# A two-layer hybrid trunk on one core: its instructions ordered by the context's timeline simulator

## The chip, the cores and the metric

The kernel runs on one core of one Trainium2 chip. The metric is the device time of one execution in microseconds; the median of several runs counts. A core has engines that run side by side, each with its own queue of instructions, which it takes in the order in which the program put them there: PE multiplies matrices (PEld is its weight load), ACT computes activations and copies, DVE does elementwise work, POOL does a little of that, and SP issues DMAs. An instruction that waits for another engine holds up what stands behind it in its own queue.

## The reference

Two decoder layers over 256 tokens of width 1024, all in float32. Cut to what matters:

```python
for l in range(2):
    x = layer_norm(ALPHA * x + swiglu_half(x, ffn1_w1[l], ffn1_w3[l], ffn1_w2[l]), ln1_g[l], ln1_b[l])
    h = x @ w_in[l]                                   # columns for three token mixers
    out_a = spatial_gating(gelu(a_u), gelu(a_v), ...)
    out_b = gated_deltanet(b_qkv, b_z, b_beta, b_decay, ...)   # short conv, triangular solve, recurrence
    out_c = gla(c_q, c_k, c_v, c_r, c_g, ...)                  # chunked recurrence
    mix = concatenate([out_a, out_b, out_c], axis=-1) @ w_out[l]
    x = layer_norm(ALPHA * x + mix, ln2_g[l], ln2_b[l])
    x = layer_norm(ALPHA * x + swiglu_half(x, ffn2_w1[l], ffn2_w3[l], ffn2_w2[l]), ln3_g[l], ln3_b[l])
# swiglu_half(x, w1, w3, w2) = 0.5 * ((silu(x @ w1) * (x @ w3)) @ w2), inner width 2816
```

## The kernel before

The activations live in SBUF as `x`, transposed: 8 blocks of 128 features by 256 tokens. All weights come from HBM as "units" of 128x1024 floats, 167 for a layer, through a ring of `raw` tiles that SP fills by DMA. Most units are split into two tiles of a narrower float: ACT casts `raw` to `wh` (L209), and DVE subtracts to get the rest, `wl` (L210). The activations are split in the same way into a high part (`xH`, or `gs` for the second FFN product) and a low part. Each 128x128 block of a unit is then three matmuls in `mm3`: `wh` by the high part (L242), `wh` by the low part (L243), `wl` by the high part (L244), 256 or 258 columns each. Units named in `whole` are used as float32 at once (L323).

A layer is FFN1, a layer norm, the mixer, a layer norm, FFN2, a layer norm. An FFN block `f` makes two products `h` (from w1 and w3), ACT and DVE turn them into `gs`, and three blocks later the products `y` (four banks of PSUM, y_0 to y_3) add the block's part of the output. PSUM has these four, and two banks each under the tags "h" and "c" for everything else.

A layer norm is spread over engines. `ln_open` adds `y` to `x` (L353) and at once makes a raw split of `x`, not yet normalised, so that PE can go on with units of the next stage whose result is corrected afterwards ("raw" products: in front of the mixer these are `pmisc`, `pm`, `pz` and `pr`; in front of an FFN, some `h`). Sums of `x` and of its square end in two matmuls `pst` (L401), and from these `ln_stats` makes the scale `rs` in a chain between ACT and DVE: `muN` (ACT, L409), its square (ACT, L410), the variance (DVE, L411 and L412), a logarithm and an exponential (ACT, both recorded as L170), and one refining step (DVE, L415 to L417). Then `x` is normalised: DVE takes off the mean (L421) and multiplies by `rs` (L425), ACT applies gain and bias (L429, `ln_x`), and `split` makes the high part (ACT, L247) and the low part (DVE, L248). The first products that use the normalised `x` are `pk` in the mixer, and `h` of a later block in an FFN. A raw product is copied out of PSUM by ACT (L629, into `zrm`), and corrected by DVE (L635, L637).

The mixer is a string of short steps on all engines between units of its own: projections (`pk`, `pq`, `pv`, each with a short convolution, L614 and L616, or by `pcv` matmuls, L680), norms of q and k (`pss`, L747), gate sums (`ptr`, L805), a triangular solve whose result is transposed on DVE (`iv`, L882 and L883), its use in small matmuls (`p1a` L899, `p2a` L905, `p1b` L919), a recurrence, and the output product.

Nothing in the code writes out the queues. `trunk` issues instructions in an order of its own, with `ahead(n)` as a priority in places. The context that it runs in (`tile.TileContext`, opened at L1346) collects them, decides in which order they stand in each engine's queue, gives them tile slots, and adds the semaphores. It picks the next instruction among those whose inputs are due by an estimate of time, and by priority.

## Time and profile before

| | us |
| --- | --- |
| median of 3 runs | 1071.11 (1066.88 to 1072.26) |
| the profiled execution | 1075.11 |
| its span, first to last instruction | 1073.3 |
| PE busy in it | 1047.1 (98%) |
| DVE busy | 749.8 (70%) |
| ACT busy | 601.4 (56%) |

The span is what the trace shows; the remaining 1.8 us lie around it. Busy shares are of the span. The granted clock of TensorE ("PEclk") is a share of its full 2.4 GHz; 0.5 is the other level, 1.2 GHz.

### The profile page before, as it was taken

What the parts mean: (1) busy time and instruction counts of PE and PEld (TensorE: products, weight loads), DVE (VectorE), ACT (ScalarE), POOL (GpSimd) and SP (SyncE); (2) the same over time, 40 slices, a digit from 0 to 9 for tenths busy, and PEclk for the clock granted to TensorE, in tenths of its full rate; (3) what the DMA queues carried; (4) which work ended last, traced back from release to release, by engine and by line L of the source; (5) the groups of instructions that cost most, each with busy time, mean ns of one, the idle gap of its engine ahead of it and who ended that gap; (6) DMA issues with size and microseconds to landing.
All of it is one profiled execution on the core that took longest, in us unless ns stands there. A gap on an engine that the chain in (4) does not pass through costs nothing.

```text
span 1073.3 us, 23703 instructions
## 1 busy us (share of the span) xinstructions
PE 1047.1 (98%) x9875; PEld 1001.9 (93%) x9875; DVE 749.8 (70%) x1324; ACT 601.4 (56%) x1063; POOL 30.6 (3%) x30
## 2 busy tenths in 40 slices
PE   8999999999899999999999999999999999999996
PEld 7999999987789999999999999999777899999995
DVE  4655556998877985556698555679898689655556
ACT  4544445686576564445566444567675765544442
POOL 0100000001020000000000000000001100000000
PEclk9999999999999999999999999999999999999998
DMA  8855557232335355556725555662324245655541
GB/s 272 300 185 193 181 190 262 98 140 95 121 100 187 102 190 191 191 194 209 258 87 193 195 197 195 221 213 93 124 83 137 79 158 193 199 194 187 190 157 40
DMA packets 51515, 182.38 MB, mean 170 GB/s; under 512 B 5840, under 2 KB 7376, under 8 KB 51280
## 3 DMA queue, kind: packets, MB, share of 16 engines
q1 hardware_dynamic: 50544, 177.23, 49.3%
q10 hardware_dynamic: 864, 3.64, 0.9%
q8 instruction: 77, 1.26, 0.5%
q14 instruction: 30, 0.25, 0.1%
HBM read 179.81 MB, written 1.05 MB: 168 GB/s over the span
## 4 chain that ended last, share of the span: by engine, by line
PE 87%; DVE 8%; ACT 3%; issue 1%; DMA 0%; DVEq 0%; SPq 0%; ACTq 0%
PE h L242 14%; PE h L243 14%; PE h L244 14%; PE y L243 6%; PE y L244 6%; PE y L242 6%; PE y L571 2%; PE y L570 2%; PE y L569 2%; DVE wl L210 2%; PE yo L243 1%; PE yo L242 1%; DVE acc L616 1%; PE yo L244 1%; PE h L323 1%
## 5 line engine op out<-in xcount | busy, mean ns | idle before, releaser
L210 DVE TENSOR_TENSOR wl<-raw,wh 128x1024 fp32r<-128x1024 f32 (+1 forms) x426 | 374.8, 898 | 196.8 <-ACT wh L209 196.3
L209 ACT CAST wh<-raw 128x1024 fp32r<-128x1024 f32 (+1 forms) x426 | 321.9, 783 | 300.0 <-issue 141.3
L242 PE MATMUL h<-x,wh 128*128 128x256 f32 x784 | 216.7, 276 | 0.0
L243 PE MATMUL h<-x,wh 128*128 128x256 f32 x784 | 216.6, 276 | 0.0
L244 PE MATMUL h<-x,wl 128*128 128x256 f32 x784 | 216.6, 276 | 0.0
L243 PEld LDWEIGHTS h<-x,wh 128*128 128x128 f32 x784 | 147.2, 188 | 0.8
L242 PEld LDWEIGHTS h<-x,wh 128*128 128x128 f32 x784 | 147.3, 188 | 0.7
L244 PEld LDWEIGHTS h<-x,wl 128*128 128x128 f32 x784 | 147.2, 188 | 0.0
L244 PE MATMUL y<-gs,wl 128*128 128x256 f32 x480 | 133.7, 279 | 0.0
L242 PE MATMUL y<-gs,wh 128*128 128x256 f32 x480 | 133.7, 279 | 0.0
L243 PE MATMUL y<-gs,wh 128*128 128x256 f32 x480 | 133.7, 278 | 0.0
L244 PE MATMUL h<-xH,wl 128*128 128x256 f32 (+1 forms) x424 | 119.6, 282 | 0.0
L242 PE MATMUL h<-xH,wh 128*128 128x256 f32 (+1 forms) x424 | 119.5, 282 | 0.0
L243 PE MATMUL h<-xL,wh 128*128 128x256 f32 (+1 forms) x424 | 119.3, 281 | 0.0
L242 PEld LDWEIGHTS y<-gs,wh 128*128 128x128 f32 x480 | 90.8, 189 | 0.0
L243 PEld LDWEIGHTS y<-gs,wh 128*128 128x128 f32 x480 | 90.2, 188 | 0.0
L244 PEld LDWEIGHTS y<-gs,wl 128*128 128x128 f32 x480 | 90.2, 188 | 0.0
L242 PEld LDWEIGHTS h<-xH,wh 128*128 128x128 f32 x424 | 81.1, 191 | 0.1
L243 PEld LDWEIGHTS h<-xL,wh 128*128 128x128 f32 x424 | 79.8, 188 | 0.1
L244 PEld LDWEIGHTS h<-xH,wl 128*128 128x128 f32 x424 | 79.7, 188 | 0.0
L475 DVE TENSOR_TENSOR g<-s,h 128x256 f32<-128x256 f32 x73 | 30.7, 421 | 41.0 <-PE h L244 40.8
L478 ACT CAST gs<-g 128x256 fp32r<-128x256 f32 x88 | 35.3, 401 | 14.6 <-DVE g L472 8.8
(441 smaller groups left out, 2167.1 us busy)
## 6 DMA issues: line engine op xcount, KB each, us to landing
raw<-w_all SPq DMA_DIRECT2D x331, 512.0 KB, 3.7
raw<-w_all SPq DMA_DIRECT2D x12, 128.0 KB, 4.5
pl<-pin ACTq DMA_DIRECT2D x2, 730.5 KB, 7.9
cst<-cin ACTq DMA_DIRECT2D x1, 1026.0 KB, 8.0
x<-xin SPq DMA_DIRECT2D x4, 256.0 KB, 4.8
out<-xT SPq DMA_DIRECT2D x4, 256.0 KB, 2.0
Gb<-gin ACTq DMA_DIRECT2D x1, 512.0 KB, 5.2
Bb<-gin ACTq DMA_DIRECT2D x1, 512.0 KB, 6.5
```

The lines of the kernel that those rows point to most:

```text
L209: st["copy"] = A.copy(WH[b][:, o:o + w], raw[b][:, o:o + w])
L210: V.tensor_sub(WL[b][:, o:o + w], raw[b][:, o:o + w], WH[b][:, o:o + w].bitcast(F32))
L242: PE.matmul(o, lhsT=wh, rhs=mh, start=first, stop=False, **kw)
L243: PE.matmul(o, lhsT=wh, rhs=ml, start=False, stop=False, **kw)
L244: PE.matmul(o, lhsT=wl, rhs=mh, start=False, stop=last, **kw)
L323: PE.matmul(h[:, o:o + T // n], lhsT=raw[b][:, k * P:(k + 1) * P], rhs=x[:, k, o:o + T // n], start=k + o == 0, stop=k == KD - 1, skip_gro ...
L475: V.tensor_mul(g, s, h3[:, :T])
L478: tab["ops"].append(A.copy(gH, g))
L569: PE.matmul(y[i], lhsT=gh, rhs=WH[b][:, s], start=n == 0, stop=False)
L570: PE.matmul(y[i], lhsT=gl, rhs=WH[b][:, s], start=False, stop=False)
L571: PE.matmul(y[i], lhsT=gh, rhs=WL[b][:, s], start=False, stop=n == NF - 1)
L616: V.scalar_tensor_tensor(acc[:, s:], p[:, :T - s], cw[:, n, 3 - s:4 - s], acc[:, s:], op0=ALU.mult, op1=ALU.add)
```

## The change

```diff
-    with tile.TileContext(nc) as tc:
+    with tile.TileContext(nc, schedule_with_timeline_sim=True) as tc:
         trunk(tc, *args, o)
```

The context picks the order of the queues by another estimate of time, its timeline simulator. Each engine gets the same instructions as before, with the same shapes: 8703 on PE, 1326 on DVE, 1071 on ACT, 35 on POOL, 353 on SP (table loads included). What differs is their order on PE, DVE and ACT, the slots that some tiles get in their pools, and with these the semaphores. POOL's order is the same, and SP's too but for one of the last output DMAs. In the long FFN stretches PE's order is the same as well. It differs around each layer norm, inside the mixers, and in the last few microseconds. In the listings, a number behind a name tells tiles of one name apart, and "x4" is four in a row.

Around the layer norm between FFN1 and the mixer of layer 0 (the one of layer 1 alike), the two `pst` matmuls move on PE from behind 53 raw matmuls (`pmisc`, `pm`, `pz`) to behind 100 of them (`pz_2436`, `pm_2462` and `pr_2494` too). The matmul after which `pk` begins has the same place in the queue. On ACT, from `muN` on, before (`pz_2436`, `pm_2462`, `pr_2494`, `pr_2526` are raw products, `rs_2408` is the logarithm, and `rs` the exponential):

```order
L409 COPY muN<-pst 128x256
L410 ACTIVATE rs_2407<-muN 128x256
L209 CAST wh_2551<-raw_2221 128x1024
L170 ACTIVATE rs_2408<-rs_2407 128x256
L629 COPY zrm<-pm_2330 128x258
L170 ACTIVATE rs<-rs_2408 128x256
L629 COPY zrm<-pz_2331 128x258
L209 CAST wh_2608<-raw_2275 128x256 x4
L629 COPY zrm<-pz_2436 128x258
L429 ACTIVATE x<-x,lnp 128x256 x8
```

And after, from the same instruction on:

```order
L409 COPY muN<-pst 128x256
L629 COPY zrm<-pz_2436 128x258
L410 ACTIVATE rs_2407<-muN 128x256
L209 CAST wh_2661<-raw_2281 128x256 x2
L629 COPY zrm<-pm_2462 128x258
L209 CAST wh_2661<-raw_2281 128x256 x2
L629 COPY zrm<-pr_2494 128x258
L209 CAST wh_2704<-raw_2491 128x256 x2
L629 COPY zrm<-pr_2526 128x258
L209 CAST wh_2704<-raw_2491 128x256 x2
L170 ACTIVATE rs_2408<-rs_2407 128x256
L170 ACTIVATE rs<-rs_2408 128x256
```

The copies of the last three raw products, which stood behind `ln_x`, now stand ahead of the logarithm. On DVE the subtractions of the same weight units and corrections (L635) stand ahead of L412, and six corrections (L637) between L425 and L248.

Inside the mixer several short steps move behind more of PE's own work: the last `pss` behind 8 more `pcv` matmuls, `ptr` behind 8, and the product ahead of the solve (`pa`) behind 15 `pav`. On ACT the square that `pss` reads stands behind four other steps. The small matmuls `p1a`, which read the solved `iv`, move the other way. On PE before (`pv_3310` is a projection of 24 matmuls, `pz_3493` one that needs nothing of the solve):

```order
L242 MATMUL pv_3310<-xH,wh_3270 128x256
L243 MATMUL pv_3310<-xL,wh_3270 128x256
L244 MATMUL pv_3310<-xH,wl_3271 128x256
L899 MATMUL p1a<-iv_3061,iv_3059 32x32 x64
L242 MATMUL pz_3493<-xH,wh_3282 128x256
```

And after:

```order
L323 MATMUL pv_3294<-x,raw_2927 128x256 x8
L242 MATMUL pv_3310<-xH,wh_3270 128x256
L243 MATMUL pv_3310<-xL,wh_3270 128x256
L899 MATMUL p1a<-iv_3061,iv_3059 32x32 x64
L944 MATMUL ptk<-cst,VV 64x64 x2
L244 MATMUL pv_3310<-xH,wl_3271 128x256
```

`p1a` stood behind all 24 matmuls of `pv_3310`; now it stands behind two of them, and the other 22 between it and `p2a`. (`ptk` are 16 small matmuls; most of them move ahead of `p1a`.)

Around each layer norm that leads into an FFN (three of them: into FFN2 of layer 0, FFN1 and FFN2 of layer 1), `pst` moves back by 47 to 63 raw matmuls, and ACT takes the casts of later weight units ahead of `ln_x`. Into FFN2 of layer 0, on ACT before (`x_4532` is the normalised high part, `g` and `s` belong to FFN blocks with raw products):

```order
L209 CAST wh_4989<-raw_4807 128x1024
L478 CAST gs<-g 128x256
L209 CAST wh_5035<-raw_4839 128x1024
L429 ACTIVATE x<-x,lnp 128x256 x2
L247 CAST x_4532<-x 128x256 x2
L209 CAST wh_5068<-raw_4869 128x1024
L429 ACTIVATE x<-x,lnp 128x256
L170 ACTIVATE s<-t_4999,cc 128x256
```

And after:

```order
L209 CAST wh_5035<-raw_4839 128x1024
L209 CAST wh_5068<-raw_4869 128x1024
L170 ACTIVATE s<-t_4875,cc 128x256
L376 CAST xH<-lnp 128x8x2
L429 ACTIVATE x<-x,lnp 128x256 x4
L247 CAST x_4532<-x 128x256
L209 CAST wh_5098<-raw_4931 128x1024
L247 CAST x_4532<-x 128x256 x3
```

Before, four of the eight blocks of `x` had been normalised ahead of the cast of `wh_5035`, and six ahead of that of `wh_5068`; after, none is ahead of either. At the end of the program the last y_0 and y_1 matmuls stand behind six more of y_2, and DVE adds y_2 to the output ahead of the statistics of y_0 and y_1.

## Rows read from the trace of the kernel before

**Rows 1.** The page: the span, and busy time of each engine.

```profile
span 1073.3 us, 23703 instructions
PE 1047.1 (98%) x9875; PEld 1001.9 (93%) x9875; DVE 749.8 (70%) x1324; ACT 601.4 (56%) x1063; POOL 30.6 (3%) x30
```

**Rows 2.** PE's waits: line, releaser, total us, times, longest.

```profile
PE h L323 <- DMA x<-xin: 5.0, 1, 5.0
PE p2a L905 <- issue: 3.4, 2, 1.8
PE pv L244 <- DVE wl L210: 3.1, 2, 1.5
PE yo L243 <- DVE mAC L248: 1.9, 2, 1.0
```

**Rows 3.** Windows of 27 us: length, then busy of PE, PEld, DVE, ACT, POOL, PEclk, DMA.

```profile
189.00:216.00 27.00, 27.00 (x223) 26.73 (x222) 25.55 (x53) 18.11 (x40) 0.00 (x0) 1.00 0.28 99
...
216.00:243.00 27.00, 26.76 (x225) 24.10 (x226) 25.81 (x69) 21.66 (x61) 0.00 (x0) 1.00 0.40 143
...
270.00:297.00 27.00, 23.36 (x511) 21.18 (x512) 22.67 (x65) 14.78 (x38) 0.00 (x0) 0.94 0.38 119
...
783.00:810.00 27.00, 23.27 (x356) 20.57 (x354) 25.31 (x73) 21.17 (x44) 0.00 (x0) 1.00 0.40 129
```

**Rows 4.** Timeline of PE: start, duration, engine, line, what; layer norm into mixer 0.

```profile
202.16 0.67 PE L401 MATMUL pst<-q,cst 128*128 128x256 f32 x2
...
216.76 0.28 PE L244 MATMUL pr<-xH,wl 128*128 128x258 f32 x1
216.88 0.28 PE L242 MATMUL pk<-xH,wh 128*128 128x256 f32 x1
217.00 0.28 PE L243 MATMUL pk<-xL,wh 128*128 128x256 f32 x1
```

**Rows 5.** Timeline of ACT at the same place; square brackets tell idle time before.

```profile
203.29 0.37 ACT L409 COPY muN<-pst 128x256 f32<-128x256 f32 x1 [3.96 <-PE pst L401]
...
205.69 0.41 ACT L170 ACTIVATE rs<-rs 128x256 f32<-128x256 f32 x1
...
210.92 4.06 ACT L429 ACTIVATE x<-x,lnp 128x256 f32<-128x256 f32 x8 [2.09 <-DVE x L425]
...
217.59 0.63 ACT L629 COPY zrm<-pr 128x258 f32<-128x258 f32 x2
218.12 1.02 ACT L209 CAST wh<-raw 128x256 fp32r<-128x256 f32 x3
```

**Rows 6.** Timeline of DVE at the same place.

```profile
209.19 0.42 DVE L417 SCALAR_TENSOR_TENSOR rs<-rs,rs 128x256 f32<-128x256 f32 x1
...
211.06 1.89 DVE L425 TENSOR_TENSOR x<-x,rs 128x512 f32<-128x512 f32 x3
...
214.65 0.76 DVE L637 TENSOR_TENSOR zrm<-zrm,rs 128x256 f32<-128x256 f32 x2
...
215.72 1.43 DVE L248 TENSOR_TENSOR xL<-x,xH 128x256 fp32r<-128x256 f32 x4
```

**Rows 7.** Timeline of all engines in mixer 0, a run of `pcv` matmuls.

```profile
249.71 1.13 PE L680 MATMUL pcv<-raw,x 128*128 128x256 f32 x4
```

**Rows 8.** Timeline of all engines around the end of the solve, mixer 0.

```profile
273.85 1.07 DVE L882 STREAM_TRANSPOSE iv<-iv 128x512 f32<-128x512 f32 x1 [0.39 <-ACT iv L881]
...
274.95 0.71 DVE L883 STREAM_TRANSPOSE iv<-iv 128x512 f32<-128x512 f32 x1
...
279.93 1.25 PE L899 MATMUL p1a<-iv,iv 32*32 32x32 f32 x122
```

**Rows 9.** Windows of 3 us behind `p1a`; columns as in rows 3.

```profile
285.00:288.00 3.00, 3.00 (x98) 2.94 (x98) 2.59 (x8) 0.00 (x0) 0.00 (x0) 0.55 0.16 63
288.00:291.00 3.00, 3.00 (x49) 2.70 (x48) 1.45 (x5) 1.46 (x5) 0.00 (x0) 0.88 0.36 113
```

**Rows 10.** Timeline of all engines, layer norm into FFN2 of layer 0, first use.

```profile
392.12 0.28 PE L242 MATMUL h<-x,wh 128*128 128x256 f32 x1
```

## Prediction

> **What bounds the kernel now.** I read the busy shares first: PE is busy for 1047.1 of 1073.3 us [rows 1]. The change takes no instruction away, so at best it removes PE's idle time, some 26 us. The list of PE's waits says where that lies: 5.0 us for the first DMA, and then 3.4, 3.1 and 1.9 us in all at three steps that belong to the two mixers [rows 2]. Behind PE's last matmul come about 9 us of output work. So what an order can win is the waits in the mixers, about 12 us in all, 1.1% of the time. The windows show that the layer norms, where nothing waits on PE, are the tight places: in 189 to 216 us and the next 27 us PE is busy for 27.00 and 26.76, but DVE for 25.55 and 25.81 [rows 3]. DVE has no room there, and what comes late on it stays late. In the FFN stretches DVE needs about half of its time, and PE's order doesn't change there; I cost them at nothing.
>
> **The layer norm into a mixer (twice).** Before, `pst` starts at 202.16 [rows 4], `muN` at 203.29, the logarithm at 205.69 [rows 5], the last refining step ends at 209.19 + 0.42 = 209.61, and the first low part of the normalised `x` is there 0.42 us after 215.72 [rows 6], at 216.14. PE asks for it at 217.00 with its second `pk` matmul [rows 4]. The slack is 0.86 us, on a chain of 14 us.
>
> Now `pst` stands behind 47 more raw matmuls. One of them takes 216.88 - 216.76 = 0.12 us [rows 4], so the statistics start 5.6 us later. That alone would use up the slack and cost 4.8 us. It gets worse on ACT: four copies of raw products and eight casts stand between `muN` and the logarithm, and the last copy waits for the raw product that ends just before `pk`, at 216.76 + 0.28 = 217.04 [rows 4]. So the logarithm can't start before about 217.04 + 0.4 for the copy + two casts of 1.02 / 3 = 0.34 [rows 5] = 218.1, which is 12.4 us later than 205.69. From there: before, 3.9 us from the logarithm's start to 209.61 [rows 5, 6]; now no casts stand between these steps on DVE, and I take 2.5, to 220.6. Four L425 in a row take 1.89 / 3 = 0.6 us each [rows 6], to 223.0; ACT's `ln_x`, 4.06 / 8 = 0.51 us a block [rows 5], runs beside it. On DVE six corrections L637 of 0.76 / 2 = 0.38 us [rows 6] and one shorter step stand next, some 2.4 us with their overlap, to 225.4, and the first L248, 1.43 / 4 = 0.36 [rows 6], ends at 225.7. PE arrives at that matmul at 217.0 + 0.6 (five others have been moved ahead of it) = 217.6. So PE, which waited for nothing here, waits about **8 us**. Bounds: 4.8 us, if the copies come earlier than I think, and 9.5 us, if the blocks behind the first trickle.
>
> **The mixer behind it (twice).** The projections of four units are then interleaved on PE, and hold all PSUM banks of "h" and "c"; `pk`, the first, is done 23 matmuls later in the queue than before. The unit that needs its bank comes at most 23 x 0.12 = 2.8 us late, and not at all if others fill the time: I take the middle, 1.3 us, bounds 0 and 2.8.
>
> The solve comes next. Its result `iv` is ready at 274.95 + 0.71 = 275.66, and `p1a` uses it at 279.93 [rows 8]: 4.3 us to spare. After, the chain to it starts 8 + 1.3 us late, and its own steps are late by some 3.8 more: `pss` and `ptr` stand behind 8 float32 `pcv` matmuls of 1.13 / 4 = 0.28 each [rows 7], 2.2 us, and `pa` behind 15 `pav` of 0.12, 1.8. So `iv` is ready at 288.8. From the start of `pk` to `p1a` PE takes 279.93 - 216.88 = 63.0 us [rows 4, 8], some 5 of them waits. After, 22 matmuls of `pv_3310` (2.6 us) stand behind `p1a` and 16 small ones of `ptk` (about 1.1) ahead, so 1.5 less work: PE would be there at 216.9 + 8 + 1.3 + 56.5 to 61.5, that is 282.7 to 287.7. It waits until 288.8, and `p1a` starts 8.9 us later than before. The two delays are not added: the solve's chain decides, and PE's first wait lies within it.
>
> Behind `p1a`, PE has 2.6 us of `pv_3310` still to do and has done 1.1 of `ptk`: +1.5. These matmuls now stand in front of `p2a`, and cover a wait of 1.8 us [rows 2]: -1.8. In the recurrence less is left to put between its steps: 0 to +3, and I take 1.4, half, since before nearly no waits are listed there and the only one near is that at `yo` with 1.0 [rows 2]. Together 8.9 + 1.5 - 1.8 + 1.4 = **10 us a mixer**, 20 for both. Ends: 5 (the solve's steps hardly late, only the 4.8 of the statistics) and 15 (8.9 + 1.5 + 3, and 1.5 more of late blocks and banks).
>
> **The clock.** After the waits at `p1a` and `p2a` the granted clock is 0.55 in 285 to 288 and 0.88 in the next window [rows 9]: 2.7 + 0.7 us at the lower level, in which half of the work is lost, 1.7 us. Before this happens once a mixer. A wait of 8 us at `pk` makes a second such stretch; I add nothing, because PE, 1.7 us slower, still comes to `p1a` ahead of 288.8. If the solve is not the bound, it is +1.7 a mixer. The Trainium skill ("TensorE: Matmul & The Clock Gate", Part 1) has it that an idle TensorE falls back to 1.2 GHz and that activity has to release it; by that rule the 8 us are sure to cost a slow start, and by the row it is likely.
>
> **The layer norm into an FFN (three times).** `pst` is 47 to 63 matmuls later, 5.6 to 7.6 us, and ACT has the casts of later units ahead of `ln_x`. Before, the normalised `x` is first used at 392.12 [rows 10], when ACT has just ended the last of its splits. After, the first block is normalised behind a cast that six blocks were ahead of. A block costs ACT 0.51 [rows 5] and a split of about 0.3, six of them 4.9, so the last blocks are up to 4.9 us later than PE's first use can stand; but PE takes them one after another, and the first is about in time. I take 2 us each (nearer to nothing, since `y` work of other blocks stands between), with bounds of 0 and 4.9: **6 us**.
>
> **The end.** y_0 and y_1 come six matmuls of 512 columns later, each twice 0.12 us [rows 4], 1.4 in all, of which DVE gives a part back: **1 us** (0.5 to 1.4). At the start only the order of the first products changes, and they wait for DMA.
>
> **The sum.** 20 + 6 + 1 = 27 us on the profiled 1075.1, 1102. That execution lies 4.0 us above the median of 1071.1; against the median it is **1098 us**. Lower ends together: 1071 + 10 + 0 + 0.5 = 1082; upper ends: 1071 + 30 + 14.7 + 1.4 = 1117.
>
> **Rivals.** (1) *Nothing net.* The order only shifts who waits, and what is done early is given back: casts and corrections which DVE does ahead of L425 aren't due later, where it has 25.8 of 27 us to do [rows 3]. For it: the same work, and the 12 us of mixer waits as a reserve. Against it: 0.86 us of slack against 5.6 us that are simple arithmetic. It decides if `pst` or the copies wait for less than I read. 1071 to 1076, say 1073. (2) *Faster.* One mechanism: the 22 matmuls in front of `p2a` fill its waits, and a simulator that sees ACT's and DVE's queues fills those at `pv` and `yo` too [rows 2]; if `iv` comes no later than PE's arrival at `p1a`, half of the 12 us are won. Price -6: 1065. It needs the chain into the mixer to be less than 1 us late. (3) *It spreads.* A late norm empties PE's store of other work; in 270 to 297 and 783 to 810 PE idles for 3.6 and 3.7 of 27 us already, with DVE at 22.7 and 25.3 [rows 3]. If the recurrence, too, runs bare, a mixer costs 18 and each FFN norm 4 or 5: 36 + 13 + 1 = 50, 1121. (4) *The clock counts in full.* Every new wait, five of them, is followed by a stretch like that of [rows 9], and nothing absorbs it: 5 x 1.7 = 8.5 on top, 1106. [...] That the change does nothing isn't possible: the queues differ.
>
> **Chances.** The forecast 0.66, nothing net 0.08, faster 0.05, spread 0.12, clock in full 0.09. The range: 1073 to 1121 leaves out the faster case, half of nothing net, half of the spread and a little of the tails of the forecast, under 0.2. About 0.5% (5.4 us) is what a measurement of this kernel can tell from no change: faster by more than that 0.05, within it 0.09, slower by more 0.86.
>
> **What would show it.** In the profile after, a wait of PE at `pk` L243 (about 8 us, twice), released by DVE's L248, with the logarithm right behind a copy of `pr`; a wait of some 5 us at `p1a`, twice, with that at `p2a` gone; and PEclk under 1.00 in the windows behind `pk`. PE's busy time stays, but for matmuls at the low clock. At each of the three FFN norms a wait of about 2 us at `h` or `y`. I am wrong if PE doesn't wait at `pk`, or if `iv` comes in time for `p1a` in spite of it. Then most of the 20 us is gone.

## The result, and the profile after

The changed kernel takes 1137.35 us (median of 4, 1133.09 to 1139.81), the kernel before 1068.99 us beside it: a ratio of 1.061, 95% interval 1.057 to 1.065. It is 68 us slower; forecast were 27. The direction was right, and the size lies outside the range.

The page of the changed kernel, span and busy times (columns as in [rows 1]):

```profile
span 1133.9 us, 23735 instructions
## 1 busy us (share of the span) xinstructions
PE 1053.6 (93%) x9875; PEld 1007.5 (89%) x9875; DVE 749.6 (66%) x1324; ACT 600.8 (53%) x1063; POOL 25.5 (2%) x30
```

PE's waits in it, as in [rows 2] (line, releaser, total, times, longest):

```profile
PE pk L242 <- ACT xH L247: 14.3, 2, 7.2
PE pqb L585 <- ACT sqb L583: 11.9, 3, 5.9
PE ptk L944 <- DVE kd L954: 7.7, 4, 3.4
PE pz L242 <- DVE acc L616: 6.5, 2, 3.7
PE p1a L899 <- DVE iv L882: 4.5, 2, 2.3
...
PE pav L685 <- ACT gu L170: 3.7, 2, 1.8
PE pS L1120 <- DVE u L1110: 3.6, 4, 1.0
PE yo L242 <- ACT mAC L247: 3.0, 2, 1.6
```

DVE and ACT are as busy as they were. What grew most is PE's idle time, from 26.2 to 80.3 us (span less busy time), 48 of these 54 us in the two mixers. The same 27 us windows as in [rows 3] have moved a little, but show it. Before, with two that [rows 3] doesn't have:

```profile
297.00:324.00 27.00, 26.95 (x532) 23.09 (x527) 20.19 (x51) 20.62 (x45) 6.20 (x3) 1.00 0.30 100
324.00:351.00 27.00, 26.03 (x247) 24.65 (x246) 21.53 (x40) 16.38 (x36) 2.63 (x4) 1.00 0.54 185
```

And after:

```profile
189.00:216.00 27.00, 22.24 (x183) 21.92 (x181) 23.12 (x52) 13.49 (x36) 0.00 (x0) 0.99 0.32 102
216.00:243.00 27.00, 24.59 (x182) 23.52 (x183) 24.42 (x65) 19.82 (x51) 0.00 (x0) 0.82 0.27 85
...
270.00:297.00 27.00, 17.79 (x401) 16.01 (x399) 24.68 (x72) 17.59 (x32) 0.00 (x0) 0.94 0.33 107
297.00:324.00 27.00, 24.18 (x442) 21.48 (x442) 18.08 (x47) 16.25 (x36) 3.21 (x3) 0.87 0.28 96
324.00:351.00 27.00, 20.56 (x334) 17.60 (x330) 15.64 (x34) 15.37 (x35) 1.35 (x1) 1.00 0.16 58
```

In the first two, PE is busy for 22 and 25 us where it had 27, and in the third for 17.8 where it had 23.4. The granted clock falls to 0.82 (216 to 243) and 0.87 (297 to 324) where it was 1.00.

To see where the time goes I cut each mixer into stages at PE's first or last matmul of a name, and took their lengths from the trace, as means of the two mixers (their totals differ by 0.2 us before and by 1.8 after; in the runs below by up to 4.7):

| stage, us | before | after | more |
| --- | --- | --- | --- |
| norm: last y of FFN1 to first pk | 21.1 | 28.2 | 7.1 |
| to the solve: first pk to first p1a | 63.0 | 66.9 | 3.9 |
| behind it: first p1a to last p1b | 15.2 | 24.6 | 9.4 |
| recurrence: last p1b to first yo | 31.6 | 34.1 | 2.5 |
| output: first to last yo | 27.1 | 34.2 | 7.1 |
| mixer | 157.9 | 188.0 | 30.0 |

Two mixers make 60 us. FFN2 of layer 0 with FFN1 of layer 1 takes 1.0 us more, FFN2 of layer 1 2.5, and what comes behind PE's last matmul 2.6. In these two traces FFN1 of layer 0 was 5.6 us shorter, which has nothing to do with the change (the last section). The sum is the difference of the spans, 60.6 us.

Of the 30.0 us more in a mixer, 24.1 are idle time of PE (6.1 before, 30.2 after). The other 5.9 are busy time, with the same matmuls. The granted clock shows where: in mixer 0 it is at 0.50 from 285.3 to 288.7 us before, and from 215.5 to 225.7, 287.2 to 290.6, 297.4 to 304.3 and 352.0 to 358.9 after, each time around or behind a wait of PE.

### The profile page after: what moved, and what is told of

The parts are those of the page before. It is cut to its first block, busy times and chain, and to the rows that moved or that the text cites. A ratio compares the mean times of both kernels' runs of the same rounds, so it can differ in the third digit from the quotient of the medians.

```text
span 1133.9 us, 23735 instructions
## 1 busy us (share of the span) xinstructions
PE 1053.6 (93%) x9875; PEld 1007.5 (89%) x9875; DVE 749.6 (66%) x1324; ACT 600.8 (53%) x1063; POOL 25.5 (2%) x30
## 4 chain that ended last, share of the span: by engine, by line
PE 80%; DVE 11%; ACT 4%; DMA 3%; issue 1%; SPq 0%; DVEq 0%; ACTq 0%
PE h L244 13%; PE h L243 13%; PE h L242 13%; PE y L242 5%; PE y L244 5%; PE y L243 5%; DMA raw<-w_all 3%; DVE wl L210 3%; PE y L569 2%; PE yo L242 1%; PE y L570 1%; PE yo L243 1%; PE y L571 1%; PE yo L244 1%; PE pcv L680 1%
## 5 line engine op out<-in xcount | busy, mean ns | idle before, releaser
L210 DVE TENSOR_TENSOR wl<-raw,wh 128x1024 fp32r<-128x1024 f32 (+1 forms) x426 | 369.3, 892 | 229.2 <-ACT wh L209 225.9
L244 PE MATMUL h<-x,wl 128*128 128x256 f32 x784 | 215.5, 276 | 0.0
L243 PE MATMUL y<-gs,wh 128*128 128x256 f32 x480 | 131.6, 277 | 0.0
L244 PE MATMUL y<-gs,wl 128*128 128x256 f32 x480 | 130.9, 277 | 0.0
L242 PE MATMUL y<-gs,wh 128*128 128x256 f32 x480 | 129.7, 277 | 1.2 <-ACT gs L478 1.2
L478 ACT CAST gs<-g 128x256 fp32r<-128x256 f32 x88 | 35.3, 401 | 11.6 <-DVE g L475 6.2
```

Source lines behind the costliest of these rows:

```text
L210: V.tensor_sub(WL[b][:, o:o + w], raw[b][:, o:o + w], WH[b][:, o:o + w].bitcast(F32))
L242: PE.matmul(o, lhsT=wh, rhs=mh, start=first, stop=False, **kw)
L243: PE.matmul(o, lhsT=wh, rhs=ml, start=False, stop=False, **kw)
L244: PE.matmul(o, lhsT=wl, rhs=mh, start=False, stop=last, **kw)
L478: tab["ops"].append(A.copy(gH, g))
```

## The experiments

Since each engine gets the same instructions, any two orders can be joined: up to a place take the one, from there the other. A function at the end of the program does that, with each instruction of PE, ACT and DVE chained behind the one that a list puts ahead of it, as issue order alone, without a wait. In the lists below a time is a place in the trace of the kernel whose order runs up to it. At a joint, what the second order would have done by then and the first has not comes first; that can make waits that neither order has by itself. The ratios are against the kernel before on the same chip.

Theory 1: the late norm is the cause, and all that waits inside the mixer is its echo. Theory 2: each stage loses by its own order.

**r1, the order alone.**

```diff
     with tile.TileContext(nc) as tc:
         trunk(tc, *args, o)
+        pin(tc)   # the order of the changed kernel, all of it
```

> The default scheduler, with the instructions of PE, ACT and DVE chained in the order that the changed kernel has (issue order alone, no added waits). It separates the order from everything else that the other scheduler decides (the slots of tiles, semaphores, SP's last DMAs). If the order alone is the cause: the time of the changed kernel, about 1137 us, ratio 1.063 (1.055 to 1.07). If slots or semaphores carry part of it: between 1069 and 1130.

1138.6 us, ratio 1.061 (1.054 to 1.068). Mixers of 187.7 us, and in them the same waits to 0.4 us. The order is the whole cause; slots and semaphores, which the default scheduler chose here, have no part that can be seen.

**r2, the norm alone, and r3, all but the norm.**

```diff
 r2: before to 170 us
+    after  to 219 us        (layer 1: before to 696, after to 774.6)
     before to the end
 r3: after  to 165 us
+    before to 217.5 us      (layer 1: after to 720, before to 742.8)
     after  to the end
```

> The order of before, but in the layer norm that leads into each mixer (from the last blocks of FFN1 to the first pk matmul) the order of the changed kernel. Theory 1 (the late norm is the cause, and the waits inside the mixers are its echo): at least two thirds of the 68 us, 1114 us or more. Theory 2 (each stage costs by its own order what its waits show): in the changed kernel this stage takes 28.2 us from the last y to the first pk in place of 21.1, in both mixers, so +14 us, 1083 us, ratio 1.013; up to 3 us more if the low clock behind the wait isn't absorbed.

> The order of the changed kernel, but in the same layer norms the order of before. Theory 1: most of the loss is gone, 1090 us or less, and the waits of PE at pqb, ptk, pz and p1a shrink with it. Theory 2: 14 to 17 us less than the changed kernel, 1120 to 1123 us, and these waits stay as they are (pqb 5.9 us in each mixer).

r2: 1090.4 us, ratio 1.016 (1.010 to 1.022), some 20 us for 14.3 us of waits. r3: 1133.2 us, 1.057 (1.050 to 1.064), so by the medians undoing it gives back 5 us of 68. The two intervals overlap, and the long FFN stretch between the mixers takes 5 us more in r3's trace than in r1's; by the mixers r3 gives back 9.7 (182.9 us in place of 187.7, twice). Either way theory 1 falls. But theory 2 in its plain form isn't right either, since 20 alone and 5 to 10 in company aren't the same. The stages say why. In r2 the norm costs 7.1 us a mixer and the stage behind it 3.2 more (66.2 in place of 63.0). In r3 that stage takes 69.9 where it took 67.1 in r1: PE comes there earlier and waits there instead.

```profile
PE pq L242 <- DVE acc L616: 4.3, 2, 2.7
...
PE pk L242 <- ACT zrm L629: 3.0, 2, 1.5
```

These are waits of PE in r3; in the changed kernel pq waits for 1.4 in all, and pk for no zrm. The wait for `zrm` is in neither whole order: it comes with the joint, where the late copies of the old norm meet the new order of the projections. So a part of what r3 doesn't give back is the joint's: 1.5 us a mixer at `pk`, and at most 1.4 at `pq`.

The 3.2 us behind the norm in r2 are the clock: in that stage PE idles for 2.7 us there (2.8 before) and is busy for 3.4 us more with the same matmuls. In the changed kernel, behind the same wait, windows of 3 us (PEclk is the last column but two):

```profile
216.00:219.00 3.00, 0.59 (x2) 0.59 (x3) 3.00 (x8) 3.00 (x7) 0.00 (x0) 0.50 0.12 49
219.00:222.00 3.00, 3.00 (x11) 2.13 (x11) 3.00 (x11) 3.00 (x9) 0.00 (x0) 0.50 0.02 5
222.00:225.00 3.00, 3.00 (x16) 3.00 (x16) 2.56 (x7) 1.18 (x4) 0.00 (x0) 0.50 0.00 0
225.00:228.00 3.00, 3.00 (x25) 3.00 (x25) 2.23 (x5) 1.93 (x2) 0.00 (x0) 0.88 0.00 0
```

PE is busy again from 218.4 on, at 1.2 GHz until 225 and a little beyond: 11 and 16 matmuls in windows that hold 25 later.

**r8, PE's part of the norm.** As r2, but ACT and DVE keep the order of before.

```diff
 before to 170 us
+PE: after to 219 us; ACT, DVE: before to 217.5 us
 before to the end
```

> The order of before, but in the norm into each mixer PE alone takes the order of the changed kernel (pst behind 47 more raw matmuls); ACT and DVE keep theirs. The prediction has 5.6 us of delay less 0.86 of slack: 4.8 us a mixer, 1079 us, up to 1083 with the low clock behind it. If the copies ahead of the logarithm on ACT are what counts, PE's order alone costs next to nothing, 1069 to 1072 us.

1083.8 us, ratio 1.011 (1.007 to 1.015), with this wait:

```profile
PE pk L242 <- ACT xH L247: 7.6, 2, 3.8
```

So the later `pst` makes 3.8 of the 7.2 us, and, by difference, ACT and DVE the other 3.4. With the low clock and what follows, it costs 7.4 us a mixer.

**r4, recurrence and output alone, and r6, the solve alone.**

```diff
 r4: before to 295 us
+    after  to 377.2 us      (layer 1: before to 820.5, after to 934.5)
     before to the end
 r6: before to 217.5 us
+    after  to 309.4 us      (layer 1: before to 742.8, after to 866)
     before to the end
```

> The order of before, but from the last p1b matmul to the end of yo (recurrence and output product) in both mixers the order of the changed kernel. Theory 1: nothing, 1069 us, since nothing is late when this stage begins. Theory 2: this stage takes 68.0 and 68.6 us in the changed kernel in place of 58.7 and 58.6, so +19 us, 1088 us, ratio 1.018, with a wait of about 5.9 us at pqb in each mixer.

> The order of before, but from the first pk to the last p1b matmul in both mixers the order of the changed kernel. That stage takes 90.9 and 92.0 us there in place of 78.1 and 78.3. With r2, about 3 us of it in each mixer are the low clock behind the wait at pk, which is not here. Theory 2 (each stage by its own order): +20 us (17 to 26), 1090 us, with waits at ptk, pz and p1a of PE. Theory 1 (echo of the late norm): 1069 to 1075 us.

r4: 1100.1 us, ratio 1.025 (1.016 to 1.033); mixers of 170.3 us, 12.4 more than before. r6: 1107.1 us, 1.032 (1.029 to 1.036); mixers of 175.3, 17.4 more. Nothing is late ahead of these stages, and each loses more than I had read off the changed kernel (17 to 26 us were expected of r6, 19 of r4). Every stage has a cause of its own. The losses of r2, r4, r6 and r7 together make 7.9%, against 6.1 for all at once. In part, what one stage loses the next needn't wait for again; in part, the joints add waits. At the first joint of r6, ten steps of ACT (eight casts, two copies of `pr`) and thirteen of DVE that the changed order has done by then come first, and PE waits as in r3 (pk for `zrm` 3.1 us in all, pq 4.7). In r4 the recurrence takes 39.0 us where it took 34.1 in r1. So 12.4 and 17.4 are upper figures for these stages' own order; the wait at `pqb` (5.7 us in r4, 5.8 in r1) is far from any joint.

**r7, the FFN stages and the end.**

```diff
 before to 353.6 us          (layer 1: after to 720, before to 879)
+after  to 720 us
 ...
+after  to the end
```

> The order of before in all of both mixers and the norms into them; the order of the changed kernel in the FFN stages with the norms that lead into them, and at the end. In the changed kernel these stretches take 1.0, 2.5 and 2.6 us more: +6 us, 1075 us, ratio 1.006. If their waits are shared with the mixers behind them: nothing.

1077.4 us, ratio 1.006 (1.002 to 1.009): as expected.

**r12 and r13, the two halves of the solve.**

```diff
 r12: before to 217.5 us
+     after  to 285.5 us     (layer 1: before to 742.8, after to 841.7)
      before to the end
 r13: before to 275.5 us
+     after  to 309.4 us     (layer 1: before to 800.6, after to 866)
      before to the end
```

> The order of before, but from the first pk matmul to the end of the solve (iv) in both mixers the order of the changed kernel. In r6, the stage to p1a took 6 to 8 us more and that from p1a to the last p1b 9.5 more. If the chain to the solve is late by its own order (pss, ptr and pa behind other work of PE): 6 to 8 us a mixer, 1084 us. If what is lost there is only PE's idle time that the second half would have had anyway: under 3 us a mixer, 1075 us.

> The order of before, but from the end of the solve to the last p1b in both mixers the order of the changed kernel. If the second half loses by its own order (subtractions of later units ahead of short steps): 7 to 10 us a mixer, 1087 us, with the waits at ptk and pz as in r6. If it is the echo of a late first half: under 3 us a mixer.

r12: 1094.7 us, ratio 1.021 (1.016 to 1.027); mixers of 167.9 us, 10 more. r13: 1083.1 us, 1.011 (1.005 to 1.018); mixers of 161.9, 4 more. Both halves lose on their own, the first more than the 6 to 8 that were expected, the second less than the 7 to 10. The first half's 10 has the waits of the joint in it, 1.5 us a mixer at `pk` and at most 1.7 at `pq`:

```profile
PE pq L242 <- DVE acc L616: 4.9, 3, 3.2
...
PE pk L242 <- ACT zrm L629: 3.1, 2, 1.6
```

r13's joint has no such backlog on DVE and one step of it on ACT; its wait at `pz` is that of r1 (6.5 us in all), and at `ptk` it has 5.2 of r1's 7.7. The first half's chain begins with the norms of q and k. The `pss` matmuls, 16 records for the eight in the two mixers, before and after (count, durations, start of the first and of the last):

```profile
L747 PE MATMUL pss<-sqkq,cst x16: 592/604/617, 235.9 to 774.4; 128*32 128x512 f32 x16
```

```profile
L747 PE MATMUL pss<-sqkq,cst x16: 592/605/617, 246.2 to 813.7; 128*32 128x512 f32 x16
```

The first stands 19.0 us behind the start of `pk` before, and 27.8 after (30.4 in r12, without the norm's delay). Before, the first two of the four `pss` of a mixer ran among the matmuls of `pq`; now all of `pq` and half of the `pkk` products are ahead of the first. From there the delay goes through `ptr` to the solve: `iv` ends 58.8 us behind the start of `pk` before, 67.2 in the changed kernel, 69.8 in r12 (mixer 0).

**r9 and r14, the solve, with DVE's subtractions and ACT's casts behind the short steps.** What the second half does in the changed kernel, DVE's timeline:

```profile
291.47 0.75 DVE L210 TENSOR_TENSOR wl<-raw,wh 128x256 fp32r<-128x256 f32 x2
292.14 0.42 DVE L901 TENSOR_TENSOR iv<-p1a,cst 128x256 f32<-128x256 f32 x1
292.47 1.76 DVE L210 TENSOR_TENSOR wl<-raw,wh 128x256 fp32r<-128x256 f32 x5
294.14 0.48 DVE L616 SCALAR_TENSOR_TENSOR acc<-pv,pl,acc 128x254 f32<-128x254 f32 x1
...
295.47 0.68 DVE L954 TENSOR_TENSOR kd<-ptk,kds 128x512 f32<-128x512 f32 x1
```

and PE's:

```profile
296.30 0.33 PE L944 MATMUL ptk<-cst,VV 64*64 64x64 f32 x4 [2.94 <-DVE kd L954]
```

Seven subtractions of later weight units stand in these lines ahead of `kd`, and PE has nothing to do from 293.4 us until `kd` is done. On ACT a convolution step stands behind four casts that wait for their DMA:

```profile
291.74 1.32 ACT L209 CAST wh<-raw 128x256 fp32r<-128x256 f32 x4 [3.20 <-DMA raw<-w_all]
292.97 0.47 ACT L614 ACTIVATE acc<-pv,pl 128x256 f32<-128x256 f32 x1
```

r9 and r14 take the order of the changed kernel and move the subtractions on DVE (`wl_3519`, `wl_3595`, `wl_3751` are the units 91 to 93) and these casts on ACT, in both mixers; PE's order stays.

```diff
 ACT:
+L614 acc<-pv, L170 VV<-acc
 L209 wh<-raw x4
-L614 acc<-pv, L170 VV<-acc
 DVE (L995 and L996 left out):
 L616 acc<-pv_3294 (1st)
+L953, L954 kb, kd<-ptk
+L616 acc<-pv_3294 (2nd, 3rd)
+L901 iv<-p1a x2                       (r14 only; r9 has it behind wl_3336)
 L210 wl_3336 x4
-L210 wl_3519 x4, wl_3595 x4, wl_3751 x4
 L907, L909, L908 on p2a, L616 acc<-pv_3310
+L210 wl_3519 x4, wl_3595 x4, wl_3751 x4
```

> The order of the changed kernel (as in r1). In the solve stage of each mixer the twelve weight subtractions of units 91 to 93 on DVE go behind the short steps that the changed order has behind them (kb and kd, the convolution of two pv, the two steps on p2a and the transposes), and on ACT one convolution step goes ahead of four casts that wait for DMA. PE's order is untouched. If casts ahead of short steps are the cause there: the waits at ptk (2.9 and 3.4 us) and pz (2.8 and 3.7) shrink to under 1, p1b starts 5 to 6 us earlier, and the time falls by 11 us or a little more with the clock, 1126 us. If PE's own order decides (ptk and 24 pz matmuls ahead of p1b): under 4 us, 1135 us or more.

> As r9, and on DVE the two steps on p1a (L901), for which PE waited 3.1 us at p2a in r9, go ahead of the four subtractions of unit 90. If the stage is a chain of short steps that each must be ahead of DVE's subtractions: the wait at p2a goes, the stage from p1a to the last p1b takes 17 to 20 us in place of 22.2 and 19.9 in r9, and the time is 4 to 5 us under r9. If PE's order decides: as r9.

r9: 1133.2 us, ratio 1.057 (1.048 to 1.065); r14: 1134.2 us, 1.060 (1.053 to 1.066). Both intervals overlap that of r1, so the times alone don't settle it: the 11 us that were expected of r9, and 4 to 5 more of r14, are not to be seen in them. The stages show a gain. From p1a to the last p1b r1 takes 24.5 us, r9 21.0, r14 19.9; before it was 15.2. In r9 the waits at `ptk` for `kd` and at `pz` for `acc` fall away and one of 3.1 us at `p2a` takes their place, because my move had put L901 behind four more steps. In r14 that goes too:

```profile
PE p1a L899 <- DVE iv L882: 4.0, 2, 2.0
...
PE p2b L926 <- DVE iv L922: 3.5, 2, 2.1
...
PE ptk L944 <- DVE kd L954: 1.1, 2, 0.6
```

So DVE's subtractions and ACT's four casts ahead of short steps carry about half of the 9.3 us of this stage, 4.6; what share each engine has isn't separated. Another 1.5 is work that the order moved into it (22 `pv` matmuls less `ptk`). The rest, 3 us, is still there. In r14's trace PE idles 1.2 us more in this stage than before and is busy 3.6 us more. The moved work is 1.5 of this; the other 2 fit the clock, at 0.50 from 291.4 to 298.2 us, where the 22 `pv` matmuls follow each other at 0.21 us in place of 0.12. That PE's own order makes the waits which are left is argued, not shown.

**r5 and r10, the output stage.** In the changed kernel, ACT ends a copy that the next step needs at 349.2, and then this happens:

```profile
352.90 1.04 ACT L209 CAST wXA<-raw 128x1024 fp32r<-128x1024 f32 x1 [3.68 <-DMA raw<-w_all]
353.85 0.41 ACT L583 ACTIVATE sqb<-O 128x256 f32<-128x256 f32 x1
...
354.31 0.80 PE L585 MATMUL pqb<-sqb,cst 128*128 128x256 f32 x1 [5.91 <-ACT sqb L583]
```

A weight cast waits for its DMA, the square stands behind it, and PE waits for the square. r5 takes that cast out of the way on ACT and its subtraction on DVE; r10 also moves two earlier subtractions behind the steps ahead of the split.

```diff
 ACT (r5, r10):
-L209 CAST wXA<-raw
 L583 sqb<-O
 L247 CAST mAC<-mc
+L209 CAST wXA<-raw
 DVE (r10; r5 has the split alone ahead of wAT):
+L589 tc, L592 mc, L248 mAC<-mc
 L210 wqd, L210 wXP
-L589 tc, L592 mc
 L210 wAT<-raw,wXA
-L248 mAC<-mc
```

> The order of the changed kernel (as in r1), with one move in the output stage of each mixer: the weight cast that waits for its DMA there (wXA on ACT, 3.7 and 2.7 us idle for it) and its subtraction on DVE go behind the square that PE waits for at pqb and behind the split of mc. If a cast that waits for DMA holds up the short steps, and that decides: PE's wait at pqb falls from 5.8 and 5 us to about 1, and the time by 8 us, 1130 us. If the next step is late as well (mc on DVE ends at 352.1, 2.3 us before yo starts; 1.3 us in the second mixer): the wait moves from pqb to yo, and only 3 to 4 us are gained, 1135 us. If the order of ACT has no part in it: 1138 us.

> As r5, and on DVE the two subtractions (wqd, wXP, 2.3 us) also go behind tc, mc and its split. In r5 the square ahead of pqb waited 2.2 us for tc. If casts ahead of short steps are the cause in the output stage: PE's wait at pqb falls to about 1.3 us in each mixer, the stage from the first to the last yo matmul takes 29 to 30 us in place of 34, and the time falls by 8 to 9 us, 1130 us. If PE's order is (pqb ahead of matmuls that covered it): the wait stays above 3 and the time within 3 us of r1.

r5: 1137.3 us, ratio 1.061 (1.054 to 1.067). The wait at `pqb` falls from 11.5 us in all to 8.6, and the stage from 33.9 us to 31.9: the square then waits 2.2 us for `tc` on DVE, because its tile isn't free. r10: 1136.3 us, 1.057 (1.048 to 1.067), with

```profile
PE pqb L585 <- ACT sqb L583: 5.3, 3, 1.8
```

and a stage of 30.1 us, against 27.1 before. Wait and stage went nearly as expected (1.8 us at most, 30.1 us), but the time fell by 2 us where I had put down 8 to 9: both mixers together are 5 us shorter in the traces, and the FFN stages together take 4.7 us more in r10's than in r1's (the last section). By the stages, casts and subtractions ahead of short steps carry more than half of what the output stage loses.

**r11, three repairs together** (r3, r9 and r10).

```diff
-after's norm, DVE's subtractions and ACT's casts as above
+before's norm into each mixer, and the moves of r9 and r10
```

> The order of the changed kernel with three repairs: the norm into each mixer in the order of before (r3), and the moves of r9 and r10. If the three causes are separate and add up: 1138 - 5 - 11 - 8 = 1114 us. If they cover each other, so that each repair alone is partly taken up by the next wait: less, down to 1100 us. If what is repaired is given back at the next step of PE's own order: 1122 us or more.

1119.0 us, ratio 1.043 (1.036 to 1.050): 20 us less than r1, and mixers of 177.0 us in place of 187.7. Measured by the stages, the repairs add up: 4.8 + 2.7 + 2.5 = 10 us a mixer by themselves, 10.7 together. The 24 us of the expectation were too much by what I had put down for r9 and r10. It is the best of the repaired orders, and by its ratio still 46 us slower than the kernel before. No order here beats that one.

## Why the prediction was wrong, step by step

**The bound** was read rightly: nothing to win beyond PE's 12 us of waits, and DVE tight around the norms. Nothing was won.

**The norm into the mixer** was right, in place and in size: a wait of 8 us was forecast, 7.2 is measured, twice, released by the normalised `x` (its high part, one matmul earlier than I had said). At `p1a`, where some 5 us were forecast, PE waits 2.3, twice. ACT's timeline after, at the place of [rows 5]:

```profile
204.14 0.37 ACT L409 COPY muN<-pst 128x256 f32<-128x256 f32 x1
...
208.39 0.38 ACT L629 COPY zrm<-pr 128x258 f32<-128x258 f32 x1 [1.03 <-PE pr L244]
211.15 0.71 ACT L209 CAST wh<-raw 128x256 fp32r<-128x256 f32 x2 [2.38 <-PE pr L243]
211.77 0.36 ACT L629 COPY zrm<-pr 128x258 f32<-128x258 f32 x1
212.03 0.71 ACT L209 CAST wh<-raw 128x256 fp32r<-128x256 f32 x2
212.65 0.86 ACT L170 ACTIVATE rs<-rs 128x256 f32<-128x256 f32 x2
```

From `muN` to the logarithm there were 2.4 us, now 8.5; it comes right behind the copy and casts of the last `pr`, as worked out, and 12.5 us later against the last y of FFN1, where I had 12.4. From there it took 5.8 us to `pk`, where I had 7.6 to the first low part. Of `pst` alone I had expected 4.8 us; r8 shows 3.8.

**The clock** is a step that failed. I added nothing for a second low stretch, because PE would still come to `p1a` before the solve was done. In r2 each wait of 7.2 us costs a mixer 10.5, and in the changed kernel the waits behind the norm bring a mixer two or three more low stretches than it had. Rival 4, the clock in full, had the sign right, but its 8.5 us were too few: in r1, where FFN1 takes as long as before, PE is busy for 1059.9 us in place of 1047.1 with the same matmuls. That is 12.8 us more, 11.6 of it in the two mixers, where I had put 0. The Trainium skill's rule in "TensorE: Matmul & The Clock Gate", Part 1, says that activity has to release the low level; the windows behind the wait agree, with PEclk at 0.50 while PE was busy for 3.00 of 3.00 us.

**To `p1a`** the sum held, for partly wrong reasons. `p1a` starts 10.6 us later (mixer 0, against the last y of FFN1); I had 8.9. For the banks and the solve's own steps I had 1.3 and 3.8 us; in the changed kernel `iv` ends 8.4 us later behind the start of `pk` than before (mixer 0), and some 3 of these are the low clock (3.6 and 2.8 in r2, which has the old order there). I had counted from the last `pss`: it is the first `pss` that moved, and the order in front of it I had not looked at. Two figures were also misread. 2.2 and 1.8 make 4.0, not 3.8, and the 2.2 is too little: a `pcv` matmul leaves two records in the trace (32 a mixer, for 16 in the code), so that eight of them are 16 records, 0.22 us apart in the changed kernel, 3.5 us. And of the 5 us of waits that I took off PE's way from `pk` to `p1a`, the trace before has 2.8. (That one decides nothing, since `iv` comes later.) The two parts cover each other, as I had said: the norm alone makes `p1a` 10.3 us late (r2), the solve's order alone 7.0, joint included (r12), both together 11.0 (means of two mixers).

**Behind `p1a`** lies the step that broke the forecast. I had +1.5 for moved work, -1.8 for a covered wait, and +1.4 for a recurrence with less to put between its steps: 1.1 us a mixer. Measured are 9.4 + 2.5 + 7.1 = 19.0. The bound, +3, was set by the waits of the kernel before, as if the order there could only lose its cover. The prediction followed only the order of PE there. What it missed is the order of ACT and DVE: subtractions of weight units that PE needs later stand ahead of `kd`, of the convolutions that free a PSUM bank, and of the steps on `p2a`; and casts that wait for a DMA stand ahead of a convolution and of the square for `pqb`. r14 and r10 take part of this back by moving just those (4.6 and 3.8 us a mixer in their stages, of which 4.8 and 2.5 show in the whole mixer); r4 and r13 show that these stages lose with nothing late ahead of them. Of the 19.0 us, 14 are idle time of PE and 5 busy time, the moved work and the clock. The covered wait, -1.8, was right (`p2a` waits for 0.2 us in all); that it was then paid for at `ptk` is argued, not shown.

**The norms into an FFN and the end** were forecast at 6 + 1 and measured at 3.5 + 2.6; r7, which has them alone, is 6 us slower by its ratio.

So 68 - 27 = 41 us were missing, and 2 x 18 of them lie behind `p1a`. Rival 3, that it spreads, named the place (the recurrence runs bare) and came nearest with 1121 us, but its mechanism, a late norm that empties PE's store of work, is theory 1, which fell.

## What to carry to other kernels

When a scheduler moves everything, read the new order of each engine from end to end against the trace, above all ACT and DVE: for each short step that PE waits for, count what stands ahead of it in its own queue, and ask of each of these whether it waits for a DMA or a slot. An order that keeps every engine's sum of work can still cost 6%. Losses of neighbouring stages cover each other, so that undoing one gives back less than it costs alone (by the stages some 10 us against 21 here, a part of which the joint makes): take each stage by itself as well as out of the whole, and look for waits that only the joint of two orders makes. And price each new wait of PE with the low clock behind it (10.5 us for 7.2 here).

## What the runs showed of the hardware

FFN1 of layer 0 takes either 190 or 196 us up to the last y, with either order (190.2 in the changed kernel, 196.5 in r1, with the same order). The granted clock is 1.00 in both. Windows of 27 us of the changed kernel, and of r1:

```profile
54.00:81.00 27.00, 27.00 (x241) 27.00 (x240) 14.53 (x16) 12.07 (x17) 0.00 (x0) 1.00 0.59 195
```

```profile
54.00:81.00 27.00, 27.00 (x231) 27.00 (x230) 14.09 (x17) 11.78 (x16) 0.00 (x0) 1.00 0.59 186
```

PE does 241 matmuls in the one and 231 in the other, 4% fewer, and is busy all the time. The stretch between the mixers, of two FFN stages, takes 367 to 368 us in ten traces and 373 or 378 in six. All six have the changed kernel's order in these stages; three others that have it too (the changed kernel, r1 and r7) are among the ten, so the order alone doesn't make it, and whether it has a part isn't known. FFN1 moves a time by 6 us, and this stretch by up to 10. Neither need be the whole of the spread, up to 15 us for one kernel: in the runs of the kernel before beside r1, the mean granted clock goes with the time too, from 0.997 at 1065.9 us to 0.988 at 1079.2. So single medians here don't tell differences of under 5 us. Why the pace differs isn't known.
